# A hybrid attention step: in three units the small sample batch is taken through at chunks 2 and 4 of its own unit

## The chip, the cores and the metric

The kernel runs on one core of a Trainium2 chip. The metric is the device time of one execution in microseconds (us). The time before is 1618.91 us, the median of three runs (1616.3 to 1619.94).

## The reference

One layer of a streaming encoder. 2048 frames of a new stream (the prompt) and 32 frames of a running one (the sample, with 256 cached frames) go through the same steps:

```
h  = rmsnorm(x) * norm_gain
qa, ka, va, ga, qb, kb, vb, gb = split(h @ w_in)          # 8 x 512 columns
oa = softmax(qa ka^T / 8 + rel_bias) va                    # A: 8 heads x 64, own chunk of 64 and the 8 before
ob = (softmax(q1 k1^T / 8) - lam * softmax(q2 k2^T / 8)) vb   # B: 4 heads x 2 x 64, block-causal
ob = rmsnorm(ob) * subln_gain * (1 - lambda_init)
y  = x + concat(oa * silu(ga), ob * silu(gb)) @ w_out
y  = rmsnorm(y) * final_gain
```

q and k of B get a partial rotary. The sample's q attends to its cached keys and values and its own 32 new ones. The outputs are y of both streams and the new cache rows. Everything is float32.

## The kernel before, in words

The mixing width is cut into eight units of 128 columns: units 0 to 3 are A (two heads each), units 4 to 7 are B (one head each). They run in the order 0, 4, 5, 1, 6, 2, 7, 3, so the A units at places n = 3, 5 and 7 are units 1, 2 and 3. A unit goes over the 2048 frames in eight chunks of 256 (c = 0 to 7). A chunk's steps are the projection of q, k, v and gate (`chunk_qkv`, L342), the scores and softmax (`attn_a` or `attn_b` up to their `yield`), and, one chunk later, the product with v (`finish`, which runs the rest of the generator). Precision is kept by splitting each float32 operand into a high and a low part, so a projection is three matmuls for each k (L296 to L298, L303 to L305).

The sample goes through `sample_unit` (L616 on) once in each unit. It is a generator with two parts. The first projects the 32 rows (L310, L311: 16 matmuls of 512 columns) and stores the new cache rows. The second loads the cached keys and values and, for A, the bias (L631 to L637), transposes (L640 to L643), forms the scores (L650), the softmax (L655 to L664), transposes the probabilities (L669), multiplies by v (L676, L678) and leaves the unit's share in `oTs` (L687 to L690). `oTs` is read by row tile 16 of the output projection alone, the last one.

After the units the output projection runs over 17 row tiles t: t = 0 to 15 are the prompt's, 16 is the sample's. Each has two halves of 512 columns; a half is 24 matmuls (L296 to L298, the same lines as in the units, here `z_ps<-w,hT` of 128x512), an add of the x rows that were loaded into `y` (L789, added at L798), a square with its sum on ScalarE (L800), then the norm and the store (L808, L809). `load_T` (L288, L289) brings the attention output of two row tiles, 2 x 1 MB.

Buffers that matter: PSUM has two `z` buffers (all projections), three `s`, two `t` and one `o`. In SBUF the tag "e" has 16 buffers of 128x512. From it come the softmax tiles of B, the raw weight pieces `wraw` that are loaded while an A unit runs (L167), five tiles of an A sample (`kvs`, `bsm`, `kTs`, `es`, `pTs`; a B sample has no `bsm`), the two `fg`, and the `y` and `sqf` tiles of the output projection. The raw pieces of both halves of w_out are 16 "e" tiles; each is given back when its split into high and low part is done (L186, L187). That split needs a free buffer of tag "w" (first half) or of "ks" and "vt" (second half), which the last unit gives back as it goes on.

The order of the instructions on each engine isn't the program's. The kernel is built under a planner (`schedule_with_timeline_sim=True`): it simulates time, takes what is ready by priority (the place in the program, moved by `ahead(n)`), hands out buffers as it goes, and fixes one order for each engine and for SP's queue of transfers. On the chip every engine and SP then go through their lists in that order, each waiting for semaphores.

Of the kernel before, what the change touches and what calls it, by code (L numbers as in the profile page):

```python
# [21 lines left out]
NCH = NT // 2  # L22
# [8 lines left out]
def hybrid_step(  # L31
# [61 lines left out]
    def e_tile(name):  # L93
        return pool.tile([P, 512], F32, name=name, tag="e", bufs=16)

    def row_tiles(name):
        return [e_tile(name + "0"), e_tile(name + "1")]

    def st_tile(name, n, bufs=4):
        return pool.tile([P, n], F32, name=name, tag=name, bufs=bufs)  # L100
# [10 lines left out]
    def z_psum():  # L111
        return psum.tile([P, 512], F32, name="z_ps", tag="z", bufs=2)
# [32 lines left out]
    def dma_here(**kw):  # L145
        tc.keep_in_program_order(SP.dma_start(**kw))

    def small_loads():
        dma_here(out=ropec, in_=rope_c)
        dma_here(out=ropes, in_=rope_s)  # L150
        dma_here(out=gcol, in_=subln)
        DVE.tensor_scalar(gcol, gcol, 1.0 - LAMBDA_INIT, 0.0, ALU.mult, ALU.add)
        lt = e_tile("lt")
        lv = lt[:, 0:256].rearrange("p (a e) -> p a e", a=4)
        dma_here(out=lt[:, 0:256], in_=lams.broadcast_to([P, 256]))
        lp = lt[:, 256:384].rearrange("p (a e) -> p a e", a=2)
        DVE.tensor_tensor(lp, lv[:, 0:4:2, :], lv[:, 1:4:2, :], ALU.mult)
        ls = st_tile("ls", 2, 1)
        DVE.tensor_reduce(ls, lp, AX.X, ALU.add)
        le = st_tile("le", 2, 1)  # L160
        ACT.activation(le, ls, AF.Exp)
        DVE.scalar_tensor_tensor(nlam, le[:, 1:2], LAMBDA_INIT, le[:, 0:1], ALU.subtract, ALU.subtract)
        ACT.copy(out=lamc[NS:2 * NS], in_=nlam[NS:2 * NS])
# [6 lines left out]
    def load_w(wsrc, cur_b, gain=None, tags=(("w", 10),) * KT, raws=None):  # L170
        his, los = [], []
        for k in range(KT):
            raw = raw_w(wsrc, k, cur_b) if raws is None else raws[k]
            tag, bufs = tags[k]
            w = pool.tile([P, 2, 512], F32R, name="w", tag=tag, bufs=bufs)
            hi, lo = w[:, 0, :], w[:, 1, :]
            g = 1.0 if gain is None else gain[:, k:k + 1]
            if raws is not None:
                ACT.activation(hi, raw, AF.Copy, scale=g)  # L179
                DVE.scalar_tensor_tensor(lo, raw, g, hi.bitcast(F32), ALU.mult, ALU.subtract)  # L180
            elif cur_b and gain is not None and k % 2 == 0:
                ACT.activation(hi, raw, AF.Copy, scale=g)
                POOL.tensor_scalar(raw, raw, g, 0.0, ALU.mult, ALU.add)
                POOL.tensor_tensor(lo, raw, hi.bitcast(F32), ALU.subtract)
            else:
                POOL.tensor_scalar(hi, raw, g, 0.0, ALU.mult, ALU.add)  # L186
                DVE.scalar_tensor_tensor(lo, raw, g, hi.bitcast(F32), ALU.mult, ALU.subtract)  # L187
            his.append(hi)
            los.append(lo)
        return his, los  # L190
# [37 lines left out]
    def load_xT(c, js=range(4)):  # L228
        xs = [e_tile("xT").rearrange("p (k t) -> p k t", k=2) for _ in js]
        for x, j in zip(xs, js):  # L230
            SP.dma_start(out=x, in_=x_t[c, :, 2 * j:2 * j + 2, :])
        return xs

    def load_rows(c):
        return [load_x(x_pv[t * P:(t + 1) * P, :], P) for t in (2 * c, 2 * c + 1)]
# [40 lines left out]
    def make_hTs():  # L276
        h = norm_rows(load_x(x_sv, NS), NS)
        tp = t_psum()
        for k in range(KT):
            j = k % 4  # L280
            PE.transpose(out=tp[:, k * NS:(k + 1) * NS], in_=h[k // 4][0:NS, j * P:(j + 1) * P], identity=ident[0:NS, 0:NS])
        tv = tp[:, 0:KT * NS].rearrange("p (k t) -> p k t", k=KT)
        ACT.copy(out=hTs[:, :, 0:NS], in_=tv)
        DVE.tensor_tensor(hTs[:, :, NS:2 * NS], tv, hTs[:, :, 0:NS].bitcast(F32), ALU.subtract)

    def load_T(src):
        hT = ht_tile()
        SP.dma_start(out=hT[:, 0].bitcast(F32), in_=src[:, 0].bitcast(F32))  # L288
        SP.dma_start(out=hT[:, 1].bitcast(F32), in_=src[:, 1].bitcast(F32))  # L289
        return hT  # L290
# [16 lines left out]
    def project_s(T, W, zp):  # L307
        his, los = W
        for k in range(KT):
            PE.matmul(zp[0:2 * NS], T[:, k, :], his[k], start=(k == 0), stop=False)  # L310
            PE.matmul(zp[0:2 * NS], T[:, k, :], los[k], start=False, stop=(k == KT - 1))  # L311
# [385 lines left out]
    pend_s = None  # L697

    def finish(gen, late):
        try:  # L700
            gen.send(late)
        except StopIteration:
            pass
# [10 lines left out]
    def get_hT(i):  # L714
        if i >= len(steps):
            return None
        n, c = steps[i]
        if n == 0:
            hT = make_hT(c, xts.pop(c))
            return hT  # L720
        return load_T(hT_d[c]), load_scales(c)
# [6 lines left out]
    for i, (n, c) in enumerate(steps):  # L728
        u = order[n]
        isB = u >= 4  # L730
        W = Ws[n]
        if c == 0:
            kss, vts = [], []
            bias = None
            if not isB:
                bias = pool.tile([P, 2, BAND], F32, name="bias", tag="bias", bufs=1)
                dma_here(out=bias, in_=bias_p[:, 2 * u:2 * u + 2, :])
                POOL.memset(bias[0:64, :, BAND - 64:BAND], NEG)
                POOL.memset(bias[64:128, :, 0:64], NEG)
        qkv = chunk_qkv(u, isB, c, hTn, W, kss, vts)  # L740
        QH, QL = next(qkv)
        gate = None
        if n == 0 and c + 2 < NCH:
            xts[c + 2] = load_xT(c + 2), load_rows(c + 2)
        hTn = get_hT(i + 1)
        if n == 0 and c == 1:
            small_loads()
        if n == 1 and c == 1:
            dma_here(out=aksv[0:PAST - NS, :], in_=cakv[NS:PAST, :])
            dma_here(out=avsv[0:PAST - NS, :], in_=cavv[NS:PAST, :])  # L750
        if n == 0 and c == NCH - 3:
            make_hTs()
        if c == NCH - 1 and n + 1 < len(order):
            v = order[n + 1]
            Ws[n + 1] = load_w(w_in[v // 4, v % 4], isB, ngain)
        prev = pend
        pend = attn_b(u, c, kss, vts, QH, QL) if isB else attn_a(u, c, kss, vts, QH, QL, bias)
        next(pend)
        late = (next(qkv), vts[c])
        if prev:  # L760
            finish(prev, plate)
        plate = late
        if c == 0:
            for _ in pend_s or ():
                pass
        if c == NCH - 2:
            pend_s = sample_unit(u, isB, W)
            next(pend_s)
    W0 = load_w(w_out[0], order[-1] >= 4)
# [5 lines left out]
        SP.dma_start(out=fg[j], in_=final_gain[:, j * 512:(j + 1) * 512].broadcast_to([P, 512]))  # L775
    oT = None
    for t in range(NT + 1):
        if t == 1:
            for _ in pend_s:
                pass  # L780
        rows = P if t < NT else NS
        yt = row_tiles("y")
        if t < NT and t % 2 == 0:
            oT = load_T(oT_d[t // 2])
        ss = st_tile("ss", 2)
        for half, W in enumerate((W0, W1)):
            cs = slice(half * 512, (half + 1) * 512)
            y = yt[half][0:rows]
            SP.dma_start(out=y, in_=x_pv[t * P:(t + 1) * P, cs] if t < NT else x_sv[:, cs])  # L789
            zp = z_psum()  # L790
            if t < NT:
                project(oT, t % 2, W, zp, slice(0, 512))
            else:
                project_s(oTs, W, zp)
                ys = e_tile("ys")
                ACT.copy(out=ys[0:NS], in_=zp[NS:2 * NS])
                DVE.tensor_tensor(y, y, ys[0:NS], ALU.add)
            DVE.tensor_tensor(y, zp[0:rows], y, ALU.add)  # L798
            sq = e_tile("sqf")
            ACT.activation(sq[0:rows], y, AF.Square, accum_out=ss[0:rows, half:half + 1])  # L800
        s1 = st_tile("ss1", 1)
        DVE.tensor_tensor(s1[0:rows], ss[0:rows, 0:1], ss[0:rows, 1:2], ALU.add)
        r = rstd_of(s1, D, rows)
        dst = y_pv[t * P:(t + 1) * P, :] if t < NT else y_sv
        for half in range(2):
            cs = slice(half * 512, (half + 1) * 512)
            y = yt[half][0:rows]
            DVE.scalar_tensor_tensor(y, y, r[0:rows, 0:1], fg[half][0:rows], ALU.mult, ALU.mult)  # L808
            SP.dma_start(out=dst[:, cs], in_=y)  # L809
# [60 lines left out]
```

## Time and profile before

| | |
|---|---|
| median of 3 runs | 1618.91 us (1616.3 to 1619.94) |
| the profiled execution | 1614.23 us |
| its span, first to last instruction | 1612.4 us |
| TensorE (PE) busy | 1547.1 us, 96% |
| VectorE (DVE) busy | 1093.3 us, 68% |
| ScalarE (ACT) busy | 1007.2 us, 62% |
| GpSimd (POOL) busy | 669.3 us, 42% |

All rows below come from the profiled execution, so a sum of them stands against 1614.23 us. That lies below the three runs (the lowest is 1616.3), and 4.68 us below their median. In a page, `out<-in` names tiles of the program, L is a line of the kernel, and "idle before <-X" says what ended the engine's wait. PEld are the weight loads that overlap PE's matmuls. The ends of matmuls are modelled; their starts are measured, so start-to-start times are used for costs.

### The profile page before, as it was taken

The page shows a single profiled execution, that of the slowest core. Times are in us where ns is not written, and L with a number is a line of the kernel's source. Part 1 is how long each engine was busy: PE and PEld are TensorE (multiplying, and loading weights), DVE is VectorE, ACT ScalarE, POOL GpSimd, SP SyncE. Part 2 cuts the span into 40 slices and gives each one's busy share as a digit, 9 for nine tenths or more (in the row PEclk, how much of TensorE's full clock was granted, in tenths as well). Part 3 has the DMA queues.
Part 4 walks back from the last instruction along what each step waited for, and adds up shares of the span by engine and source line. Part 5 has one row for each costly group of instructions (what it writes and reads, how often), then busy time and mean ns, then how long its engine had stood idle before and what let it go on. Part 6 is the DMA issues. An engine that isn't in the chain of part 4 may idle for free.

```text
span 1612.4 us, 30675 instructions
## 1 busy us (share of the span) xinstructions
PE 1547.1 (96%) x10448; PEld 1430.0 (89%) x10448; DVE 1093.3 (68%) x3045; ACT 1007.2 (62%) x2706; POOL 669.3 (42%) x1117
## 2 busy tenths in 40 slices
PE   7999999999999899999998999999999999989997
PEld 7999999898998899999997999999878899968885
DVE  5777668885788856675788667666888577743333
ACT  7885667785778766655777566556677566531111
POOL 5565424653346534353446344443454344510000
PEclk9999999999999999999999999999999999999999
DMA  9964454433432153336422453354331264334562
GB/s 363 367 231 166 158 192 138 155 107 131 149 128 88 70 196 131 137 131 211 167 83 76 148 181 132 134 180 152 136 131 70 89 248 142 128 133 162 175 211 66
DMA packets 105662, 249.67 MB, mean 155 GB/s; under 512 B 11192, under 2 KB 60480, under 8 KB 88064
## 3 DMA queue, kind: packets, MB, share of 16 engines
q1 hardware_dynamic: 105504, 247.70, 43.3%
q8 instruction: 83, 1.36, 0.3%
q14 instruction: 75, 0.61, 0.1%
HBM read 194.83 MB, written 53.75 MB: 154 GB/s over the span
## 4 chain that ended last, share of the span: by engine, by line
PE 80%; DVE 9%; ACT 4%; issue 3%; DMA 3%; POOL 1%; SPq 0%; DVEq 0%; ACTq 0%; POOLq 0%
PE z_ps L296 12%; PE z_ps L297 12%; PE z_ps L298 12%; PE t_ps L434 6%; PE z_ps L303 5%; PE s_ps L425 5%; PE z_ps L304 5%; PE z_ps L305 5%; PE s_ps L426 5%; PE o_ps L603 2%; PE o_ps L602 2%; DVE nmx L513 2%; PE o_ps L547 2%; PE o_ps L548 2%; PE o_ps L549 2%
## 5 line engine op out<-in xcount | busy, mean ns | idle before, releaser
L296 PE MATMUL z_ps<-w,hT 128*128 128x256 f32 (+2 forms) x1280 | 424.0, 332 | 12.4 <-ACT w L179 6.2
L297 PE MATMUL z_ps<-w,hT 128*128 128x256 f32 (+2 forms) x1280 | 422.4, 330 | 2.0 <-DVE w L180 1.2
L298 PE MATMUL z_ps<-w,hT 128*128 128x256 f32 (+2 forms) x1280 | 421.2, 329 | 0.0
L296 PEld LDWEIGHTS z_ps<-w,hT 128*128 128x128 f32 x1280 | 243.5, 191 | 29.8 <-ACT w L179 6.2
L297 PEld LDWEIGHTS z_ps<-w,hT 128*128 128x128 f32 x1280 | 243.7, 190 | 18.5 <-DVE w L187 2.6
L298 PEld LDWEIGHTS z_ps<-w,hT 128*128 128x128 f32 x1280 | 243.7, 190 | 13.5
L515 ACT ACTIVATE e<-s_ps,nmx 128x512 f32<-128x512 f32 (+3 forms) x320 | 199.0, 626 | 85.1 <-DVE nmx L513 81.2
L444 DVE TENSOR_TENSOR pl<-t_ps,ph 128x512 fp32r<-128x512 f32 (+1 forms) x312 | 191.9, 622 | 77.2 <-ACT ph L443 66.4
L303 PE MATMUL z_ps<-hT,w 128*128 128x256 f32 x768 | 223.3, 291 | 2.8 <-DVE ql L391 2.2
L304 PE MATMUL z_ps<-hT,w 128*128 128x256 f32 x768 | 221.9, 289 | 0.0
L305 PE MATMUL z_ps<-hT,w 128*128 128x256 f32 x768 | 221.2, 288 | 0.0
L443 ACT CAST ph<-t_ps 128x512 fp32r<-128x512 f32 (+1 forms) x312 | 162.4, 535 | 91.2 <-PE o_ps L602 45.9
L425 PE MATMUL s_ps<-ks,qh 128*128 128x512 f32 (+2 forms) x544 | 193.5, 366 | 19.6 <-ACT e L515 17.6
L513 DVE TENSOR_REDUCE nmx<-s_ps 128x1 f32<-128x512 f32 (+3 forms) x320 | 188.2, 600 | 18.9 <-PE s_ps L426 16.0
L426 PE MATMUL s_ps<-ks,ql 128*128 128x512 f32 (+2 forms) x544 | 184.1, 351 | 0.0
L521 POOL TENSOR_SCALAR e<-e,da 128x512 f32<-128x512 f32 (+3 forms) x160 | 111.5, 711 | 140.8 <-DVE da L491 114.9
L303 PEld LDWEIGHTS z_ps<-hT,w 128*128 128x128 f32 x768 | 149.4, 194 | 6.5 <-DVE ql L391 2.9
L304 PEld LDWEIGHTS z_ps<-hT,w 128*128 128x128 f32 x768 | 149.5, 195 | 3.1 <-issue 1.3
L305 PEld LDWEIGHTS z_ps<-hT,w 128*128 128x128 f32 x768 | 149.5, 195 | 1.4
L580 POOL TENSOR_SCALAR ea<-ea,sma 128x640 f32<-128x640 f32 (+4 forms) x128 | 98.2, 769 | 112.8 <-DVE sma L579 99.5
L578 ACT ACTIVATE ea<-ea,nma 128x640 f32<-128x640 f32 (+4 forms) x128 | 97.2, 760 | 61.9 <-DVE nma L576 60.8
L425 PEld LDWEIGHTS s_ps<-ks,qh 128*128 128x128 f32 x544 | 101.8, 189 | 31.9 <-ACT e L515 25.2
(205 smaller groups left out, 3374.9 us busy)
## 6 DMA issues: line engine op xcount, KB each, us to landing
hT<-hTd SPq DMA_DIRECT2D x112, 1024.0 KB, 5.6
wraw<-in_w_in_dram SPq DMA_DIRECT2D x64, 256.0 KB, 5.2
hTd<-hT SPq DMA_DIRECT2D x8, 2048.0 KB, 8.9
oTd<-oT SPq DMA_DIRECT2D x64, 256.0 KB, 3.7
hT<-oTd SPq DMA_DIRECT2D x16, 1024.0 KB, 7.8
out_dram<-z SPq DMA_DIRECT2D x160, 64.0 KB, 1.6
xT<-in_x_t_dram SPq DMA_DIRECT2D x32, 256.0 KB, 5.2
xt<-in_x_prompt_dram SPq DMA_DIRECT2D x32, 256.0 KB, 6.0
```

The lines of the kernel that those rows point to most:

```text
L296: PE.matmul(zp, hT[:, 0, k, ts], his[k][:, cols], start=(k == 0), stop=False)
L297: PE.matmul(zp, hT[:, 0, k, ts], los[k][:, cols], start=False, stop=False)
L298: PE.matmul(zp, hT[:, 1, k, ts], his[k][:, cols], start=False, stop=(k == KT - 1))
L303: PE.matmul(zp, his[k][:, cols], hT[:, 0, k, :], start=(k == 0), stop=False)
L304: PE.matmul(zp, his[k][:, cols], hT[:, 1, k, :], start=False, stop=False)
L305: PE.matmul(zp, los[k][:, cols], hT[:, 0, k, :], start=False, stop=(k == KT - 1))
L425: PE.matmul(sp[:, 0:w], QH[:, m, qs], ks[:, m, kc], start=True, stop=False)
L426: PE.matmul(sp[:, 0:w], QL[:, m, qs], ks[:, m, kc], start=False, stop=True)
L443: ACT.copy(out=hv, in_=tv)
L444: DVE.tensor_tensor(lv, tv, hv.bitcast(F32), ALU.subtract)
L513: DVE.tensor_reduce(nmx[:, m, b:b + 1], sp[:, 0:w], AX.X, ALU.max, negate=True)
L515: ACT.activation(e[:, 0:w], sp[:, 0:w], AF.Exp, bias=nmx[:, m, b:b + 1], accum_out=sm[:, m, b:b + 1])
```

## The change

For the units at n = 3, 5 and 7 (A units other than the first), the first part of `sample_unit` is emitted at chunk 2 in place of chunk 6, and the second part at chunk 4 of the same unit in place of chunk 0 of the next one. For the last unit (n = 7) the second part stood in the output projection, ahead of row tile 1; that place is taken away. Unit 0 and all B units keep chunk 6 and chunk 0 of the next unit. At chunk 0 of every unit the line that finishes a pending sample stays; behind a moved sample it finds nothing to do. No instruction is added to or taken from the program by the source; only its place, and with it the planner's order.

```diff
         plate = late
-        if c == 0:
+        mid = n > 0 and not isB
+        if c == 0 or (mid and c == 4):
             for _ in pend_s or ():
                 pass
-        if c == NCH - 2:
+        if c == (2 if mid else NCH - 2):
             pend_s = sample_unit(u, isB, W)
             next(pend_s)
...
     for t in range(NT + 1):
-        if t == 1:
-            for _ in pend_s:
-                pass
+
         rows = P if t < NT else NS
```

## Rows read from the trace of the kernel before

**Rows 1.** The page: busy time of each engine over the span (time, share, instructions).

```profile
PE 1547.1 (96%) x10448; PEld 1430.0 (89%) x10448; DVE 1093.3 (68%) x3045; ACT 1007.2 (62%) x2706; POOL 669.3 (42%) x1117
```

**Rows 2.** Busy time by stage (stretch in us from the start, its length, then busy us and instructions of PE, PEld, DVE, ACT and POOL, granted TensorE clock, DMA share, GB/s). The stages: unit 1 (A); the first chunk of unit 6 (B); the late chunks of unit 6; those of unit 7 (B); unit 3 (A, the last); the first row tiles of the output projection; the rest of it.

```profile
575.00:725.00 150.00, 149.30 (x1149) 144.04 (x1149) 98.48 (x308) 91.83 (x233) 62.81 (x131) 1.00 0.40 144
725.00:760.00 35.00, 34.59 (x231) 32.41 (x230) 18.88 (x54) 18.49 (x55) 11.60 (x24) 1.00 0.63 216
830.00:925.00 95.00, 85.99 (x605) 78.26 (x604) 74.05 (x169) 68.36 (x182) 49.05 (x65) 0.98 0.29 100
...
1180.00:1275.00 95.00, 86.36 (x595) 78.88 (x594) 75.14 (x182) 70.34 (x189) 49.98 (x69) 0.96 0.28 97
1275.00:1400.00 125.00, 124.67 (x975) 119.74 (x976) 87.94 (x266) 77.08 (x198) 57.13 (x116) 1.00 0.46 165
1423.00:1440.00 17.00, 9.92 (x46) 7.03 (x45) 6.88 (x19) 4.53 (x17) 1.99 (x3) 0.89 0.59 219
1440.00:1596.00 156.00, 155.87 (x671) 126.90 (x672) 50.62 (x126) 26.31 (x86) 0.00 (x0) 0.99 0.47 161
```

**Rows 3.** The waits of TensorE, 1400 to 1440 us (who waited, for whom: us in total, times, longest).

```profile
PE z_ps L296 <- DVE y L798: 3.4, 2, 2.6
```

**Rows 4.** TensorE in order of time, 1430 to 1444 us (start, duration, line, operation; in brackets the idle time ahead of it and what ended it). L296 to L298 are the output projection, L640 to L678 the sample of unit 3.

```profile
1430.38 0.38 PE L640 MATMUL t_ps<-ident,kvs 128*128 128x128 f32 x2
...
1435.09 0.39 PE L669 MATMUL t_ps<-ident,es 64*128 64x64 f32 x3 [2.47 <-POOL es L664]
...
1439.73 0.80 PE L296 MATMUL z_ps<-w,hT 128*128 128x512 f32 x1 [2.62 <-DVE y L798]
...
1443.28 0.40 PE L298 MATMUL z_ps<-w,hT 128*128 128x512 f32 x1
1443.51 0.40 PE L296 MATMUL z_ps<-w,hT 128*128 128x512 f32 x1
```

**Rows 5.** The chain of work that ended last, 1431 to 1440 us (start, duration, piece).

```profile
1431.43 7.53 DMA y<-in_x_prompt_dram
...
1438.98 0.70 DVE y L798
```

**Rows 6.** SP's queue in order of time (start, time to issue, line, transfer), the last unit and the tail.

```profile
1350.72 0.33 SPq L288 DMA_DIRECT2D hT<-hTd  x1
...
1368.94 0.33 SPq L288 DMA_DIRECT2D hT<-oTd  x1
...
1419.63 0.52 SPq L457 DMA_DIRECT2D oTd<-oT  x1
1420.20 0.60 SPq L631 DMA_DIRECT2D kvs<-in_cache_a_k_dram  x1
...
1427.56 0.52 SPq L457 DMA_DIRECT2D oTd<-oT  x1
1428.18 1.06 SPq L809 DMA_DIRECT2D out_dram<-y  x2
1430.58 0.33 SPq L288 DMA_DIRECT2D hT<-oTd  x1
...
1431.43 1.91 SPq L789 DMA_DIRECT2D y<-in_x_prompt_dram  x3
```

**Rows 7.** DMA issues of two stretches (transfer, count, KB each, median us from issue to landing): 1360 to 1362 us, then 1425 to 1445 us.

```profile
y<-in_x_prompt_dram SPq DMA_DIRECT2D x1, 256.0 KB, 2.5
...
hT<-oTd SPq DMA_DIRECT2D x2, 1024.0 KB, 7.3
y<-in_x_prompt_dram SPq DMA_DIRECT2D x5, 256.0 KB, 7.5
```

**Rows 8.** TensorE in order of time, first chunk of unit 6: the sample of unit 1 among other matmuls.

```profile
739.77 0.38 PE L640 MATMUL t_ps<-ident,kvs 128*128 128x128 f32 x2
...
740.37 0.44 PE L297 MATMUL z_ps<-w,hT 128*128 128x384 f32 x1
740.66 0.34 PE L298 MATMUL z_ps<-w,hT 128*128 128x384 f32 x1
...
741.94 0.39 PE L303 MATMUL z_ps<-hT,w 128*128 128x256 f32 x1
...
749.26 0.33 PE L669 MATMUL t_ps<-ident,es 64*128 64x64 f32 x2
749.52 0.44 PE L298 MATMUL z_ps<-w,hT 128*128 128x384 f32 x1
...
753.79 0.55 PE L676 MATMUL o_ps<-pTs,kvs 128*128 128x64 f32 x4
...
754.63 0.44 PE L434 MATMUL t_ps<-ident,e 128*128 128x128 f32 x2
```

**Rows 9.** When a sample fills its last "e" buffer (pTs, ACT) and when SP issues the next weight pieces (wraw): at the start of unit 1, then of unit 3.

```profile
591.26 0.27 ACT L671 COPY pTs<-t_ps 128x128 f32<-128x128 f32 x1
...
590.77 0.42 SPq L167 DMA_DIRECT2D wraw<-in_w_in_dram  x1
...
1290.88 0.27 ACT L671 COPY pTs<-t_ps 128x128 f32<-128x128 f32 x1
...
1290.39 0.42 SPq L167 DMA_DIRECT2D wraw<-in_w_out_dram  x1
...
1293.02 13.50 SPq L167 DMA_DIRECT2D wraw<-in_w_out_dram  x14
```

## Prediction

> **What bounds the kernel now.** I read the page's busy shares first, then the busy time by stage, then TensorE's waits and its order of time around the one large wait, and last the chain of work and SP's queue there. TensorE is busy 96% of the span, no other engine above 68% [rows 1]. That share is an average, and the stages differ. In an A unit TensorE does not wait: 149.30 of 150 us in unit 1, 124.67 of 125 in unit 3, and the first chunk of a B unit is nearly as full, 34.59 of 35. The late chunks of a B unit lose some 9 us each, 85.99 and 86.36 of 95. The output projection is full from 1440 on, 155.87 of 156. Only its first row tiles stand out: 9.92 busy of 17 us, at a granted clock of 0.89 [rows 2]. This is the stretch in which the sample of unit 3 is finished.
>
> There TensorE ends its projection work at 1430.38, where the sample's first transpose starts, and takes it up again at 1439.73 [rows 4]. So 9.35 us hold nothing but the sample's few matmuls. What the reader is to see is what ended the gap. It was not the sample: TensorE waited for the DVE add of a y tile [rows 3, 4], and the chain goes through the landing of that y, 7.53 us after its issue at 1431.43 [rows 5]. Both z buffers held the two halves of row tile 1 and could not be read before their x rows were there. SP's queue says why these came late: the issue stands behind the sample's loads (1420.20), the store of the last attention output, the stores of row tile 0 and a load_T of 2 x 1 MB at 1430.58 [rows 6].
>
> **Why the y load stood there.** The "e" buffers seem to be handed out in the order of the program. In unit 1 and in unit 3 the next raw weight pieces were issued within half a microsecond of the moment at which the sample filled its last "e" tile: 590.77 beside 591.26, 1290.39 beside 1290.88 [rows 9]. In the tail the five tiles of the sample stand in the program ahead of the y tiles of row tile 1. The planner filled pTs only after it had run the sample's softmax, and so it put those loads behind the load_T, which waits for the last matmul of row tile 1. This reading is inferred from rows, not shown by one.
>
> **What the change does, part by part.**
>
> 1. The tail. With the sample gone, the first y of row tile 1 takes the place in SP's queue that kvs had: 1420.20, behind the store at 1419.63 [rows 6]. A y load with free queues lands 2.5 us after its issue [rows 7], so it is there before the add needs it. The second y should follow the stores of row tile 0, that is after 1428.18 + 1.06 = 1429.24, and before the load_T at 1430.58 [rows 6]; it would land near 1432. Row tile 2 can then start at 1430.38 in the buffer of the first half, and takes 24 x 0.23 = 5.5 us for a half (0.23 is 1443.51 less 1443.28 [rows 4]). The second buffer is free by 1433, long before it is wanted. Next late is the first y of row tile 2, behind the load_T: 1431.43 + 7.5 = 1438.9. Its z is ready at 1435.9 and the buffer is wanted again at 1441.4, so that wait is covered. Removed: 9.35 us.
>
> 2. The clock. From 1439.73 to 1443.28 eight matmuls took 3.55 us, against 8 x 0.23 = 1.84 [rows 4]. They ran at 1.2 GHz after the gap and at 2.4 GHz later. Removed with the gap: 1.71 us.
>
> 3. The sample's second part in unit 3. Unit 3 has no idle time on TensorE [rows 2], so there its matmuls cost their full time. The nearest rows are those of the sample of unit 1 among other work: 739.77 to 740.37 is 0.60 us for the transposes, 740.66 to 741.94 less the 0.17 of the matmul ahead is 1.11 for the scores with a short wait, 749.26 to 749.52 is 0.26 for two of three probability transposes, so 0.39, and 753.79 to 754.63 is 0.84 for the product [rows 8]. Sum: 2.94 us. Bounds: 0, if it filled idle time that I don't see, and about 6, if each of its three handovers waited once more as the scores did. I take 2.94, since these rows are of the same code in an equally full stage.
>
> 4. Units 1 and 2. Their second part leaves the first chunk of units 6 and 7 and comes into units 1 and 2. Both stages are full [rows 2], so 2.94 us are taken away in one and added in the other: 0. The same holds for the first part (16 matmuls of 512 columns) in all three units, from chunk 6 to chunk 2 of the same unit: 0. If the B unit's first chunk had slack, the cost would be up to 2 x 2.94 = 5.9.
>
> 5. What is moved in queues. SP's list loses kvs and bsm loads at the unit boundaries and gets them in mid unit. By the order of the "e" buffers the raw weight pieces now also come later, behind the sample of chunk 4. In unit 3 their 16 issues hold SP for 1293.02 + 13.50 - 1290.39 = 16.1 us [rows 9]. Cover: they are first wanted when the last unit gives its weight buffers back, towards the end of the unit. DVE, ACT and POOL have 37, 48 and 68 us free in unit 3 [rows 2], so the sample's short operations there cost nothing. If the pieces hold up the load of the last chunk's hT, that is a rival below.
>
> Sum: -9.35 - 1.71 + 2.94 = -8.1 us. Against the profiled execution's 1614.23 that is 1606.1; its time lies 4.7 below the median of the three runs, and I forecast on the median: 1618.91 - 8.1 = 1610.8 us. The order is planned anew from unit 1 on, and the late chunks of units 6 and 7 have 9.0 and 8.6 us of waits that may fall otherwise [rows 2]; half of one of them, 4.4, is my estimate for this either way: 1606.4 to 1615.2.
>
> **The rivals.** (a) Only the first y gets ahead of the load_T. The second is then issued at 1431.4 and lands near 1439; its buffer is free at 1439.7, while row tile 2's first half ends at 1435.9. A stall of 3.8 us stays: 1614.6. For it: the margin in part 1 is only 1.3 us. By the Trainium skill (DMA: Bandwidth & Descriptors, "Queues, rings and completion order") each DMA engine takes the transfers of one issuing queue in ring order; the trace agrees, 7.5 us for a y behind the 2 MB and 2.5 alone [rows 7].
>
> (b) The slower one: the y loads stay where they are, because what delays them is the planner's place for them beside the load_T and not the sample's tiles. It decides as soon as the first y of row tile 1 is issued after the load_T at 1430.58. The gap then stays as it is, only emptier, and unit 3 pays the 2.94 of part 3, up to 6 with the further waits: 1621.9, at most 1625. Against it speak rows 9. The Trainium skill (Perfetto Trace Analysis, "Optimization Strategy") says that a kernel whose most-contended engine changes over time may gain by interleaving such regimes. By that rule the sample belonged beside the output projection, where DVE is busy 50.62 of 156 us against 87.94 of 125 in unit 3, and taking it away would cost the same 2.94. The trace speaks against the rule here: TensorE is full in both stages [rows 2].
>
> (c) The raw pieces push the load of chunk 7's hT. It was issued at 1350.72, and the unit's next buffer came free at 1368.94 [rows 6], 18.2 us later; the load needs 7.3 [rows 7], so it can be 10.9 late. Pushed by the whole 16.1, TensorE waits 5.2 us: 1616.0.
>
> (d) The change may not do what it says: if the weight pieces took all "e" buffers first, the sample of unit 3 would still be finished late in that unit. It would still be out of the tail, so the time is that of the forecast.
>
> **How the numbers follow.** Forecast, with (d): 0.62, at 1610.8. (a) 0.12 at 1614.6; (b) 0.13 at 1621.9; (c) 0.06 at 1616.0; B units planned anew by more than half their waits: 0.07, of which two thirds on the fast side. The measurement can tell about 0.2% from no change, 3.2 us, so faster is below 1615.7 and slower above 1622.1. Faster: 0.56 of the forecast's 0.62, 0.08 of (a), 0.03 of (c) and 0.04, so 0.71. Slower: half of (b) and the rest of the anew planned, 0.06 + 0.03, and 0.03 for part 4's 5.9 with the gap not fully closed: 0.12. Same: 0.17. The range goes from 1606.0 to 1619.0; it leaves out (b) and a few per cent on either side.
>
> **What would show it.** In the changed kernel: no wait of more than 1 us on TensorE between 1425 and 1445 and a granted clock of 1.00 there; the y loads of row tile 1 ahead of the third load_T in SP's queue; L640 to L678 of unit 3 between 1310 and 1365, with no TensorE wait beside them; the 16 weight pieces issued after that sample's pTs; unit 3 some 3 us longer. I am wrong in the main step if a gap of 9 us is still there, and in parts 3 and 4 if waits appear in the A units.

## The result, and the profile after

The changed kernel takes 1594.97 us (median of four runs, 1594.15 to 1595.64) against 1618.89 in the same comparison: ratio 0.9854, interval 0.9837 to 0.9871. That is 23.9 us less, three times the forecast of 8.1 and below its range. The profiled execution took 1595.64 us with a span of 1593.6, so the two profiles differ by 18.8 us of span; sums below stand against that.

The page of the changed kernel, busy time of each engine, answers to [rows 1]: TensorE is busy 5 us less, with as many matmuls, and for a larger share of a shorter span.

```profile
PE 1541.8 (97%) x10448; PEld 1431.8 (90%) x10448; DVE 1088.5 (68%) x3045; ACT 1010.3 (63%) x2706; POOL 670.1 (42%) x1117
```

Busy time by stage of the changed kernel, columns as in [rows 2]: the late chunks of unit 6, those of unit 7, the end of the last unit, the rest of the output projection.

```profile
819.00:914.00 95.00, 91.18 (x652) 84.24 (x650) 80.29 (x181) 71.51 (x188) 54.15 (x70) 1.00 0.31 106
...
1162.00:1257.00 95.00, 91.19 (x656) 84.50 (x655) 79.84 (x182) 72.55 (x190) 53.33 (x69) 1.00 0.31 109
...
1400.00:1417.00 17.00, 14.74 (x90) 12.08 (x89) 11.96 (x34) 9.94 (x26) 8.61 (x20) 0.96 0.10 32
1420.00:1577.00 157.00, 157.00 (x685) 128.17 (x684) 51.00 (x126) 25.96 (x84) 0.00 (x0) 1.00 0.52 179
```

Read the counts first. In 95 us of late chunks TensorE now does 652 and 656 matmuls, before 605 and 595, and the granted clock is 1.00 in place of 0.98 and 0.96 [rows 2]. If one matmul there is worth another, that is 95 x (1 - 605/652) = 6.8 us and 95 x (1 - 595/656) = 8.8 us: some 15.6 of the 18.8, in stages of units 6 and 7 in which no sample runs in either kernel.

What TensorE waited for there before (for whom: us in total, times, longest; first the late chunks of unit 6, then of unit 7):

```profile
PE s_ps L425 <- ACT e L515: 4.3, 6, 1.4
...
PE s_ps L425 <- ACT e L515: 4.7, 4, 2.5
```

and in the changed kernel; both stretches have these same lines:

```profile
PE z_ps L303 <- DVE ql L391: 1.7, 1, 1.7
PE s_ps L425 <- ACT e L515: 1.0, 1, 1.0
```

L515 is the exponential of B's softmax. Before, TensorE reached these chunks with the softmax behind it; now it doesn't. From the last product with v of one unit to that of the next (the start of its last L603 or L549), the two traces give these lengths in us:

| | before | after | change | forecast |
|---|---|---|---|---|
| unit 1 | 155.4 | 158.5 | +3.1 | +2.9 |
| unit 6 | 193.5 | 182.8 | -10.8 | -2.9 |
| unit 2 | 156.1 | 159.5 | +3.5 | +2.9 |
| unit 7 | 194.6 | 180.6 | -14.0 | -2.9 |
| unit 3 and all behind it | 329.0 | 325.0 | -4.0 | -8.1 |
| units 0, 4 and 5 | 583.7 | 587.2 | +3.5 | 0 |

Neighbouring units overlap, so a single row is good to a few us. The pairs are firmer: units 1 and 6 together lose 7.7 us, units 2 and 7 10.5. The 3.5 us of units 0, 4 and 5 stand where the change moves nothing.

**Where it came from.** The two "t" buffers of PSUM serve all transposes. By the rows that follow they too are handed out in the order of the program, and the sample's probabilities (L669) took one, as late as its softmax allows. Behind them in that order stand the key and query transposes of the B unit's second chunk (L370, L372). TensorE of the kernel before, unit 6:

```profile
748.47 0.27 PE L669 MATMUL t_ps<-ident,es 64*128 64x64 f32 x1
748.68 0.33 PE L370 MATMUL t_ps<-ident,z 128*128 128x128 f32 x1
748.84 0.27 PE L372 MATMUL t_ps<-ident,z 128*128 128x128 f32 x1
```

ScalarE of the kernel before, same stretch (z is what these transposes read, e what the second chunk's softmax writes):

```profile
723.72 0.58 ACT L349 ACTIVATE z<-z_ps,rsd 128x384 f32<-128x384 f32 x1
...
757.76 0.58 ACT L515 ACTIVATE e<-s_ps,nmx 128x384 f32<-128x384 f32 x1
```

z was ready at 724.3; its transposes ran at 748.68, 0.2 us after the sample's, and the first exponential 9 us later. The same 0.2 us stands in all four B units: 209.0 and 209.2 in unit 4, 400.4 and 400.6 in unit 5, 1098.4 and 1098.6 in unit 7. In the changed kernel units 6 and 7 have no A sample there. TensorE, then ScalarE of the changed kernel, unit 6:

```profile
740.98 0.27 PE L370 MATMUL t_ps<-ident,z 128*128 128x128 f32 x1
```

```profile
728.93 0.58 ACT L349 ACTIVATE z<-z_ps,rsd 128x384 f32<-128x384 f32 x1 [1.14 <-PE z_ps L298]
...
750.39 0.58 ACT L515 ACTIVATE e<-s_ps,nmx 128x384 f32<-128x384 f32 x1 [1.45 <-DVE nmx L513]
```

The transposes now run 11.5 us after their z is ready, before 24.4. They come 7.7 us earlier, the exponential 7.4; in unit 7 15.3 (1098.6 to 1083.3) and 14.9 (1107.6 to 1092.7). Counted from the last product with v of the unit before, which takes out that the units themselves start at other times, this exponential comes 4.7 us behind it in both units, 18.6 and 18.8 before. TensorE has other matmuls to do meanwhile, so no wait shows here. The price appears some 100 us later, in the waits for L515. That the late transposes cause these waits is at this point a reading; the experiments test it.

**The tail.** SP's queue of the changed kernel (start, time to issue, line, transfer; answers to [rows 6]):

```profile
1410.04 0.56 SPq L788 DMA_DIRECT2D y<-in_x_prompt_dram  x1
1417.30 0.51 SPq L457 DMA_DIRECT2D oTd<-oT  x1
1417.90 0.56 SPq L788 DMA_DIRECT2D y<-in_x_prompt_dram  x1
...
1422.90 0.33 SPq L288 DMA_DIRECT2D hT<-oTd  x1
```

TensorE of the changed kernel at the same place (answers to [rows 4]):

```profile
1415.47 0.52 PE L296 MATMUL z_ps<-w,hT 128*128 128x512 f32 x1 [1.75 <-DVE y L797]
1415.80 0.61 PE L297 MATMUL z_ps<-w,hT 128*128 128x512 f32 x1
...
1419.20 0.41 PE L296 MATMUL z_ps<-w,hT 128*128 128x512 f32 x1
```

The y loads stand ahead of the third load_T, and the 9.35 us gap is gone. What is left is a wait of 1.75, and after it eight matmuls in 1419.20 - 1415.80 = 3.40 us, 0.43 each: 1.2 GHz, where 0.23 is 2.4 GHz; the granted clock from 1415 to 1420 is 0.66. The wait ends with the add of the second half of row tile 0, whose x rows were issued at 1379.26. VectorE comes to that add straight from the last steps of the attention, so its order holds TensorE here, and no load:

```profile
1414.26 0.43 DVE L609 TENSOR_TENSOR on<-o_ps,on 64x256 f32<-64x256 f32 x1
1414.72 0.69 DVE L797 TENSOR_TENSOR y<-z_ps,y 128x512 f32<-128x512 f32 x1
```

### The profile page after: what moved, and what is told of

The parts are those of the page before. It is cut to its first block, busy times and chain, and to the rows that moved or that the text cites. A ratio compares the mean times of both kernels' runs of the same rounds, so it can differ in the third digit from the quotient of the medians.

```text
span 1593.6 us, 30646 instructions
## 1 busy us (share of the span) xinstructions
PE 1541.8 (97%) x10448; PEld 1431.8 (90%) x10448; DVE 1088.5 (68%) x3045; ACT 1010.3 (63%) x2706; POOL 670.1 (42%) x1117
## 4 chain that ended last, share of the span: by engine, by line
PE 81%; DVE 8%; ACT 4%; DMA 3%; issue 2%; POOL 2%; SPq 0%; DVEq 0%; ACTq 0%; POOLq 0%
PE z_ps L296 12%; PE z_ps L298 12%; PE z_ps L297 12%; PE t_ps L434 6%; PE s_ps L425 5%; PE s_ps L426 5%; PE z_ps L303 5%; PE z_ps L304 5%; PE z_ps L305 5%; PE o_ps L603 2%; PE o_ps L602 2%; DVE nmx L513 2%; PE o_ps L549 1%; PE o_ps L547 1%; PE o_ps L548 1%
## 5 line engine op out<-in xcount | busy, mean ns | idle before, releaser
L296 PE MATMUL z_ps<-w,hT 128*128 128x256 f32 (+2 forms) x1280 | 424.3, 332 | 11.0 <-ACT w L179 6.3
L298 PE MATMUL z_ps<-w,hT 128*128 128x256 f32 (+2 forms) x1280 | 424.6, 332 | 0.0
L296 PEld LDWEIGHTS z_ps<-w,hT 128*128 128x128 f32 x1280 | 245.5, 192 | 27.1 <-ACT w L179 6.3
L297 PEld LDWEIGHTS z_ps<-w,hT 128*128 128x128 f32 x1280 | 245.4, 192 | 15.6 <-DVE w L180 0.9
L298 PEld LDWEIGHTS z_ps<-w,hT 128*128 128x128 f32 x1280 | 245.3, 192 | 13.7 <-issue 0.4
L515 ACT ACTIVATE e<-s_ps,nmx 128x512 f32<-128x512 f32 (+3 forms) x320 | 198.8, 625 | 90.1 <-DVE nmx L513 86.5
L303 PE MATMUL z_ps<-hT,w 128*128 128x256 f32 x768 | 220.2, 287 | 4.5 <-DVE ql L391 3.3
L304 PE MATMUL z_ps<-hT,w 128*128 128x256 f32 x768 | 219.1, 285 | 0.0
L305 PE MATMUL z_ps<-hT,w 128*128 128x256 f32 x768 | 219.0, 285 | 0.0
L513 DVE TENSOR_REDUCE nmx<-s_ps 128x1 f32<-128x512 f32 (+3 forms) x320 | 187.3, 600 | 10.4 <-PE s_ps L426 7.1
L303 PEld LDWEIGHTS z_ps<-hT,w 128*128 128x128 f32 x768 | 146.6, 191 | 8.4 <-DVE ql L391 3.8
L304 PEld LDWEIGHTS z_ps<-hT,w 128*128 128x128 f32 x768 | 146.6, 191 | 2.8 <-issue 0.9
L305 PEld LDWEIGHTS z_ps<-hT,w 128*128 128x128 f32 x768 | 146.5, 191 | 2.1 <-issue 0.4
L425 PEld LDWEIGHTS s_ps<-ks,qh 128*128 128x128 f32 x544 | 101.8, 189 | 21.6 <-ACT e L515 12.6
```

The costliest lines, as they stand in the source:

```text
L296: PE.matmul(zp, hT[:, 0, k, ts], his[k][:, cols], start=(k == 0), stop=False)
L297: PE.matmul(zp, hT[:, 0, k, ts], los[k][:, cols], start=False, stop=False)
L298: PE.matmul(zp, hT[:, 1, k, ts], his[k][:, cols], start=False, stop=(k == KT - 1))
L303: PE.matmul(zp, his[k][:, cols], hT[:, 0, k, :], start=(k == 0), stop=False)
L304: PE.matmul(zp, his[k][:, cols], hT[:, 1, k, :], start=False, stop=False)
L305: PE.matmul(zp, los[k][:, cols], hT[:, 0, k, :], start=False, stop=(k == KT - 1))
```

## The experiments

The theories, in the order in which they were formed. **A**: the B unit's first softmax tiles stand behind the sample's pTs in the order of the "e" buffers. **B**: the sample's own work holds up the engines in the B unit's first chunks. **C**: the plan fell better by chance. **D**, formed when A failed as the first link: the order of the "t" banks, as told above. Each run is given with its median, the median of the kernel before in the same comparison, and the ratio with its interval. "Key transposes" are L370 of the B unit's chunk.

**Only the last unit moved.**

```diff
+        mid = n == len(order) - 1
```

> Only the last unit (n = 7) takes its sample through at chunks 2 and 4; units 1 and 2 are as before. Theory A (order of the e buffers: in a B unit the softmax tiles of the second chunk stand behind the sample's last tile, the softmax starts some 12 us later, and the late chunks pay about 10 us for it): only the tail is mended, 8 us less than before, about 1611, and units 6 and 7 keep TensorE waits of about 9 us each in their late chunks. Theory B (the sample's own work in the B unit's first chunk is what cost): also about 1611. Theory C (a new plan by chance, no tie to the sample's place): any time, and the late waits of units 6 and 7 may go although nothing was moved there.

1611.78 against 1617.18, 0.9967 (0.9951 to 0.9983). The gap is gone, and the waits for L515 in the late chunks of units 6 and 7 are as before: 4.2 and 4.4 us in the same windows. Parts 1 to 3 alone are worth some 5.4 us. By the last product with v, unit 3 is 7.6 us longer than before (147.3, 139.7) and what stands behind it 11.5 us shorter (177.9, 189.4).

**Only units 1 and 2 moved**, the last unit's sample left in the tail.

```diff
+        mid = n in (3, 5)
```

> Only units 1 and 2 are moved; the last unit's sample stays in the output projection. Theory A: units 6 and 7 start the softmax of their second chunk some 19 us after that of the first and not 31, and lose about 10 us less each: 16 us less than before in all, about 1603, with the 9 us gap of the tail still there. Theory B: the work moves from one full stage to another, so at most 3 us less, about 1616 to 1619. Theory C: no forecast.

1592.88 against the same 1617.18, 0.9852 (0.9832 to 0.9871). The whole gain of the change (0.9854). Units 6 and 7 last 179.3 and 180.6 us, before 193.5 and 194.6. So the gain is that of units 1 and 2, which I had put at zero.

**Out of the B unit, but only to the end of the A unit.**

```diff
+        mid = n > 0 and not isB
+        if c == 0 or (mid and c == NCH - 1):
             for _ in pend_s or ():
                 pass
         if c == NCH - 2:
```

> First part at chunk 6 as before, second part at chunk 7 of the same A unit (n = 3, 5, 7), so in the program it still stands ahead of the next B unit's first softmax tile, but next to it in time. Theory A: what counts is the order in the program against the B unit's tiles, so about the time of the changed kernel, 1592 to 1599. Theory B: the work lies near the same stage as before, so most of the gain in units 6 and 7 is lost: about 1608 to 1612. Theory C: no forecast.

1614.38 against 1617.18, 0.9985 (0.9973 to 0.9997). This missed what A had expected. TensorE of this kernel at the start of unit 6:

```profile
731.26 0.27 PE L669 MATMUL t_ps<-ident,es 64*128 64x64 f32 x1
731.46 0.33 PE L370 MATMUL t_ps<-ident,z 128*128 128x128 f32 x1
```

The pair of 0.2 us has moved with the sample: now the key transposes of the first chunk stand behind it, where they stood at 716.96 before. Its first exponential comes at 740.18, before at 726.96. This row points to the "t" buffers.

**The sample of B units at chunks 2 and 4 too.**

```diff
+        mid = n > 0
+        if c == 0 or (mid and c == 4) or (n == 0 and c == NCH - 1):
```

> Chunks 2 and 4 of the own unit for every unit but the first, and unit 0 finishes its sample at its own chunk 7, so no B unit has a sample in its first chunk. Theory A: units 4 and 5 gain like units 6 and 7 did, about 10 us less each, some of it given back in the units that take the work: 1575 to 1582. Theory B: work moved between full stages, within 3 us of the changed kernel: 1592 to 1597. Theory C: no forecast.

1614.67 against 1617.18, 0.9983 (0.9969 to 0.9998), so the gain is lost. ScalarE of this kernel in unit 4:

```profile
286.02 0.21 ACT L515 ACTIVATION_READ_ACCUMULATOR e<-s_ps,nmx 128x1 f32 x1
301.40 0.27 ACT L671 COPY pTs<-t_ps 128x128 f32<-128x128 f32 x1
...
308.76 0.69 ACT L515 ACTIVATE e<-s_ps,nmx 128x512 f32<-128x512 f32 x1 [2.57 <-DVE nmx L513]
```

Between the last exponential of one chunk and the first of the next lie 22.5 us, with the sample's pTs in them. A sample in the middle of a B unit holds up that unit's softmax, and by the same pair: the key transposes of the following chunk start at 299.94, 0.2 us behind the sample's at 299.74.

**The "e" order taken away.** First a control with 14 "e" buffers, then the sample's three tiles in tags of their own with the same 14, then that on the changed kernel.

```diff
-        return pool.tile([P, 512], F32, name=name, tag="e", bufs=16)
+        return pool.tile([P, 512], F32, name=name, tag="e", bufs=14)
...
-        kT = e_tile("kTs")
+        kT = pool.tile([P, SK + NS], F32, name="kTs", tag="kTs", bufs=1)
```

and `es` and `pTs` likewise (not in the control).

> The kernel before with 14 e buffers in place of 16: the control of the next run, in which two buffers had to make room. All theories: a little slower or the same, 1615 to 1630. The first softmax of a B unit's second chunk still stands 7 to 8 us behind the sample's pTs (750.1 to 757.8 before).

> As the control, with the sample where it was before, but its three late tiles (kTs, es, pTs) in buffers of their own and not under the tag e. Work, engines and PSUM are those of the control. Theory A (order of the e buffers): the softmax of the second chunk no longer waits for pTs, in units 4 and 5 too; the late chunks of units 6 and 7 lose 10 us less each and the tail gap of 9 us goes: 16 to 35 us less than the control. Theory B (the sample's work in the first chunk): the time of the control, within 3 us. Theory C (a plan by chance): no forecast.

> The changed kernel with 14 e buffers and the sample's three late tiles in buffers of their own. Theory A: units 4 and 5 may gain as well, the rest is already mended by the place: at or below the run before it, 1580 to 1596. Theory B: the gain of the change stands against the control as it did at 16 buffers, 24 us.

Against 1617.33: 1623.88, 1.004 (1.0024 to 1.0056); 1617.6, 0.9998 (0.9982 to 1.0015); 1615.2, 0.999 (0.9974 to 1.0005). In the second, the key transposes of the second chunk still stand 0.2 us behind the sample's (760.91 and 760.70), and the first exponential at 769.93. A fell as the first link. What these tags did change is the tail: from the last gate of unit 3 on, TensorE is idle for 1.9 us in the second and 7.3 in the control, and the second is 6.3 us faster than the control. That fits what the prediction inferred from [rows 9]. The third loses nearly all of the change's gain; in unit 6 its key transposes of the first chunk run 18.5 us after the start of their z and not 12, with no sample in the way. What holds them there is not settled. Where the time went can be read: of the 19.8 us of span between the third and the change, 13.4 lie in units 0, 4 and 5, whose samples the change doesn't move (600.6 and 587.2 us); the control, too, loses 9.8 us there against the kernel before.

**Priority.** The second part of the sample is pulled forward for the planner.

```diff
+            with ahead(600):
+                for _ in pend_s or ():
+                    pass
```

> The kernel before, with the priority of the sample's second part raised by 600 places at chunk 0 of the next unit; its work and its place in the program stay. Theory A: pTs is filled earlier, and the first softmax that stands behind it follows 7 to 8 us after it; if it comes more than 8 us earlier than before, units 6 and 7 lose less: 1600 to 1612. If the raised sample holds up chunk 0's softmax as in the run with the end of the unit, no gain: 1612 to 1618. Theory B: the same work in the same stage, 1616 to 1620.

1618.34 against 1617.33, 1.0013 (1.0 to 1.0026). L669 comes at 756.91 in unit 6 and the key transposes at 757.23, 0.3 us behind: priority doesn't bring the sample forward, and the order stays.

**One line, and nothing moved**: the probabilities' transposes go into a half of the sample's "o" bank that is free at that time; `op` holds the bank anyway.

```diff
-        tp2 = t_psum()
+        tp2 = op[:, 256:512]
```

> The kernel before, all places as there; only the sample's second transposes (of the probabilities, three small ones) go to the PSUM bank of its product (tag o) in place of one of tag t. Theory A (e buffers) has fallen: with own buffers the second chunk's softmax still stood 7.5 us behind pTs. Theory D (order of the two t banks): the key transposes of a B unit's second chunk stand in the program behind the sample's second transposes and were run 0.2 us after them in every unit; freed of that, they come at least 8 us earlier (by 741 in unit 6, not 748.7), the softmax with them, and the late chunks of units 6 and 7 wait less, units 4 and 5 perhaps too: 5 to 9 us less for each of two to four units, 1590 to 1607. The tail is as before. Theory B (work in place) or C (chance): 1614 to 1622.

1590.12 against 1618.08, 0.9831 (0.9814 to 0.9847). TensorE of this kernel in unit 6:

```profile
731.41 0.27 PE L370 MATMUL t_ps<-ident,z 128*128 128x128 f32 x1
...
743.27 0.39 PE L669 MATMUL o_ps<-ident,es 64*128 64x64 f32 x3
```

ScalarE of this kernel behind it:

```profile
744.90 0.26 ACT L671 COPY pTs<-o_ps 128x128 f32<-128x128 f32 x1
745.15 0.57 ACT L515 ACTIVATE e<-s_ps,nmx 128x384 f32<-128x384 f32 x1
```

What TensorE waited for L515 in this kernel, in all of unit 6, then of unit 7 (4.3 and 5.8 us before):

```profile
PE s_ps L425 <- ACT e L515: 0.8, 2, 0.6
...
PE s_ps L425 <- ACT e L515: 0.6, 1, 0.6
```

The key transposes pass the sample's in all four B units, by 9.8 to 12.3 us, and the time falls by 28 us with the sample where it was. Units 6 and 7 are 7.9 and 10.4 us shorter than before, units 4 and 5 3.6 and 2.6. D is shown in this: freeing the bank that the sample's second transposes take is enough to remove the loss, with no work moved. The ScalarE rows show the next link: the first exponential now stands 0.25 us behind pTs, so A's order of "e" buffers comes to bear as a second link, once the first is open.

**Both of the sample's transposes in the "o" bank.**

```diff
-        tp = t_psum()
+        op = o_psum()
+        tp = op[:, 0:512]
```

with `tp2` as above.

> As the run before it, and the sample's first transposes go to the same bank of tag o as well, so that the sample takes no t bank at all; the o bank is held longer, by some 15 us at the unit's start, where it lies idle. Theory D: the second chunk's key transposes are free of the sample, 12 us after their z: units 6 and 7 as in the changed kernel, 10 us less each, units 4 and 5 too if they pay for it: 1575 to 1600. Theory B or C: 1614 to 1622.

1615.57 against 1618.08, 0.9997 (0.9984 to 1.0009). A miss. The key transposes are free here as well, but the sample itself is later: its second transposes come 14.3 to 17.7 us after the last product of the unit before, with the one line 9.0 to 12.6. The first exponential (760.20 in unit 6) stands behind pTs (759.94) by the second link. And unit 1, an A unit, is 5.0 us longer than before, with one wait of 3.90 us on TensorE. So the bank alone doesn't decide; how late the sample gets does too.

**The change and the one line together; the change and both.**

> The changed kernel with the sample's second transposes in the o bank. Theory D: units 6 and 7 are free of the sample already; the samples of units 0 and 4, which still stand in the first chunk of units 4 and 5, no longer hold up those: 0 to 15 us less than the changed kernel, 1580 to 1595. Theory B or C: 1595 or worse.

> The changed kernel with all transposes of the sample in the o bank. Theory D: as the run before it or up to 5 us less; if the longer hold of the one o bank in the middle of an A unit delays its products, up to 5 us more: 1578 to 1598.

1583.97, 0.979 (0.9776 to 0.9805), the lowest of all and faster than both kernels; and 1617.98, 1.0 (0.9985 to 1.0014), a miss. The second loses the whole gain in units 1, 2 and 3, which hold the sample in their middle: 169.6, 169.6 and 152.5 us, in the change 158.5, 159.5 and 144.1. Units 6 and 7 keep theirs (182.7 each). The longer hold of the one "o" bank, for which the expectation had allowed up to 5 us, fits this; it wasn't tested apart.

**The second link lifted as well**: the es of an A sample is put into `bsm`, and pTs into the rest of `kTs`, together with the one line; on the kernel before, then on the changed kernel.

```diff
-        e = e_tile("es")
+        e = e_tile("es") if isB else bsm
...
-        pT = e_tile("pTs")
+        pT = kT[:, 320:512]
```

> The kernel before with the sample's second transposes in the o bank, and its probabilities packed into tiles that it has already: pT in the free columns of kTs, and for A units es in the bias tile. So the last e buffer that the sample takes is kTs (A) or es (B), 10 or 5 us earlier than pTs. Theory D with two links: with the t bank freed, the first exp of the second chunk stood 0.2 to 0.3 us behind pTs in eight of eight unit starts; freed of that too, it comes some 7 us after the key transposes, 4 to 7 us earlier in units 6 and 7 than with the t bank alone. If an early start goes on paying, 3 to 10 us less than that run: 1580 to 1587. If 5 us of start no longer matter: 1587 to 1593.

> The changed kernel with the sample's second transposes in the o bank and the same packing. Only units 4 and 5 still have a sample (of units 0 and 4) in their first chunk: theory D with two links gives them 3 to 5 us each at best: 1576 to 1584. If the start no longer matters: 1582 to 1586.

1595.93 against 1618.21, 0.9865 (0.985 to 0.988), and 1594.25, 0.9847 (0.9827 to 0.9866). The second link is open: in unit 6 the second chunk's exponentials begin 8.3 us after the last product of the unit before, 14.5 with the one line alone. Yet this is 6 us slower than the one line, and the second is 9 us slower than the change with the one line; both miss what was expected. That an ever earlier start goes on to pay is wrong.

**Units 1 and 2 moved, with the one line.**

> Only units 1 and 2 moved (the last unit's sample stays in the output projection), with the sample's second transposes in the o bank. Without that bank this placing gave 1592.9 against 1595.0 for the whole change, though the tail gap stays in it. If moving the last unit's sample costs its unit more than it gives the tail, this is below the whole change with the o bank, 1578 to 1583; if the tail's 8 us count in full, above it: 1586 to 1592.

1590.05 against 1618.21, 0.9826 (0.9812 to 0.9841). By the ratios, since these are of several comparisons: with the one line, moving the last unit's sample as well is worth 0.0036 (0.9826 to 0.979, 5.8 us); alone it was 0.0033, 5.3 us; in the change it is worth nothing (0.9852 to 0.9854).

**Neighbouring places, and more priority for the key transposes.** The change at chunks 3 and 5, at 1 and 3, and the best version with `ahead(300)` for `ahead(150)` at L367.

> The changed kernel with the two parts one chunk later, at chunks 3 and 5. Theory D: the sample is as far from the B unit's first chunk as before, so nothing of the mechanism changes: 1595, and whatever else comes is the scatter of the plan. If the gain hangs on chunks 2 and 4 by chance (theory C): 1605 or more.

> The changed kernel with the two parts one chunk earlier, at chunks 1 and 3. Theory D: 1595 and the plan's scatter. Theory C: 1605 or more.

> The changed kernel with the sample's second transposes in the o bank (1584.0), and the priority of a chunk's key and query transposes raised from 150 to 300 places. Unit 7 there took its first key transposes 18.6 us after their z and not 12, and its late chunks waited again. If the order of the t banks is what holds them (they stand behind the transposes of the A unit's products), they come earlier and unit 7 loses some 10 us: 1572 to 1580. If the raised place only pushes the products back: 1584 to 1600.

Against 1617.79: 1599.42, 0.9874 (0.9847 to 0.9902); 1599.7, 0.9888 (0.9868 to 0.9908); 1588.51, 0.9815 (0.9799 to 0.9831). Most of the gain is that of taking the sample out of the B unit's start, not of chunks 2 and 4: 20.4 and 18.1 us by the ratios stand at the neighbours, against 23.6. The intervals overlap, so the difference of 3 to 6 us, if it is one, may be C's, the particular plan. The third is no faster than the best version (0.979; the intervals just overlap), and in it unit 7's first key transposes still run 18.6 us after the start of their z (1041.0 to 1059.6); priority isn't what they lack.

**All kernels side by side.** In the units 6 and 7 of the twenty traces, the waits for L515 go with how late the second chunk's key transposes run after their z is ready. In the 20 units where that is 15.5 us or less, TensorE waits 0 to 2.4 us for L515, the middle one 0.8; in the 20 units where it is 16.9 us or more, 2.3 to 6.5, the middle one 4.3. This holds without a sample in the way, too: in the change with both banks, 19.8 and 20.2 us and waits of 4.3 and 4.1. The start of the exponential tells less: there it stands 3.9 and 4.2 us behind the unit before, in the one-line kernel 14.5 and 13.9, with waits of 0.8 and 0.6. So the late key transposes are the sign to go by, and the order behind the sample is one way to get them. This is a count over kernels that differ in other things too, and the waits for L515 are a part of their times alone.

## Why the prediction was wrong, point by point

**Part 4 is the step that failed**: "Both stages are full, so 2.94 us are taken away in one and added in the other: 0." The 2.94 as TensorE work were about right: units 1 and 2 grew by 3.1 and 3.5 us. But units 6 and 7 became 10.8 and 14.0 us shorter, where the step took away 2.94 each. What the step left out is who stands behind the sample. I had seen that "e" buffers go out in program order, and used it for the tail alone; the "t" banks go out in the same way, and the fullness of the first chunk says nothing of what its softmax may not yet start. I priced a place by TensorE's busy share in that place, while the cost lay in the late chunks. [rows 2] had those 9.0 and 8.6 us of waits, and I took them as noise of a new plan, with 0.07 for more than half of them. By the counts, some 15.6 us came from there.

**Parts 1 and 2** were right in mechanism. The y loads come ahead of the third load_T, the L296 gap is gone, and the tail alone is faster (the first experiment). What stands behind unit 3's last product became 11.5 us shorter there and 8.5 in the change, where 9.35 + 1.71 = 11.1 was forecast. Of the 9.35 us gap 6.3 were idle time, 5.1 of it in the two waits of [rows 4]; the rest was the sample's work, which part 3 counts again. The sign that I had asked for, no wait above 1 us and a clock of 1.00, did not come in the change: an add in the tail is awaited for 1.75 us, then the eight slow matmuls cost 8 x 0.2 = 1.6. The clock term was thus paid again, at another place.

**Part 3** was right in kind and too small: unit 3 became 4.4 us longer in the change and 7.6 with the tail alone, for 2.94. The sample of unit 3 runs at 1334 to 1353, among other matmuls and without a wait beside it. TensorE's idle time in unit 3 rose from 0.5 to 2.2 us, most of it one wait of 1.70 us at 1377.25, 24 us behind the sample; in units 1 and 2 it fell from 0.4 and 0.5 to nothing. I was to be wrong if waits appeared in the A units, and this one did. Parts 1 to 3 together were put at 8.1 us; alone they measured 5.4 (interval 2.7 to 7.9).

**Part 5** was right in the main: the 16 weight pieces are issued from 1347.3 on, beside the sample's pTs at 1349.7, so the first of them ahead of it and not behind; the load of chunk 7's hT is not pushed to a wait. Rivals (a) to (d) did not decide. Rival (b), the slower one, is refuted by SP's queue.

That "faster" came true is in good part luck. The forecast rested on the tail, and beside the moves of units 1 and 2 the tail's mending is worth nothing that can be measured (0.9852 and 0.9854); the gain came from the term that I had put at 0.

**What stays open.** Why the last unit's move is worth nothing beside the moves of units 1 and 2, and 5 to 6 us alone or with the one line. Against the kernel with units 1 and 2 alone, the change takes 2.1 us off behind unit 7 and adds 3.0 in units 0, 4 and 5 and 3.5 in unit 6, where the last unit's move touches nothing. Further: why some B units run their key transposes 18 us late without a sample; why 14 "e" buffers cost so much in units 0, 4 and 5; and why lifting the second link made the kernel slower. The planner's order is made anew with every edit, and I take that for the common reason; it is argued, not shown. The one line is 5.5 us faster without the further start that the lifted second link gives (0.9831 and 0.9865), so a few us of a single edit can't be put down to its mechanism here.

## What to carry to other kernels

Where buffers are handed out in the order of the program, list each tag that a small side task takes, PSUM banks too, and ask who stands behind it; an engine that is full there doesn't make the place free, for what is held up may set the pace of a later stage. Two unlike instructions that stand 0.2 us apart in every unit point to such a link. It may be cheaper to cut it by giving the side task another bank (here one line, 28 us) than by moving the task, but each such edit has to be measured: with both of its transposes in that bank the gain was gone. A wait that is spread over a late stage is to be followed back to the start of that stage's slowest chain before it is called noise.

## What the runs showed of the hardware that was not expected

A wait of 1.75 us in the tail, after the shorter waits of 0.15 and 0.27 us ahead of it, was followed by eight matmuls at 1.2 GHz (granted clock 0.66 from 1415 to 1420); I had looked for that only behind a gap of 9 us. The wait's length alone doesn't tell: 38 us earlier in the same trace, a wait of 1.70 us ahead of the same kind of matmul was followed by matmuls 0.23 us apart, 2.4 GHz, at a granted clock of 1.00 from 1377 to 1383.

```profile
1377.25 0.50 PE L296 MATMUL z_ps<-w,hT 128*128 128x512 f32 x1 [1.70 <-DVE ql L391]
...
1378.51 0.40 PE L298 MATMUL z_ps<-w,hT 128*128 128x512 f32 x1
1378.74 0.39 PE L296 MATMUL z_ps<-w,hT 128*128 128x512 f32 x1
```

In the first experiment a wait of 0.79 us at the place in the tail (1433.63) stood in a stretch with a granted clock of 1.00 (1399 to 1450). What sets these cases apart no run here shows.
